# A hybrid SSD and Conformer layer on one core: the issue order of all queues, up to the up projection, from a table in the source

## The chip, the cores and the metric

The kernel runs on one core of a Trainium2 chip. The metric is the device time of one execution in microseconds (us), lower being better. The core has a matrix engine (TensorE, PE in the profile), a vector engine (VectorE, DVE), an activation engine (ScalarE, ACT), a general engine (GpSimd, POOL) and a queue that issues the DMA transfers (SyncE, SP). Each of them works through its own list of instructions in order, and an instruction that needs the result of another engine waits for that engine's semaphore at the head of its list, with everything queued behind it.

## The reference

One inference step of a trunk layer over 128 context tokens and 512 latent tokens, width 1024, in float32:

```python
mod = jax.nn.silu(cond) @ prm["w_ada"] + prm["b_ada"]
sh1, sc1, g1, sh2, sc2, g2 = [m[:, None, :] for m in jnp.split(mod, 6, axis=-1)]
h = rms_norm(x, prm["norm_mix_pre"]) * (1 + sc1) + sh1
proj = h @ prm["w_in"]
z, xbc, dt_raw, cf_in = jnp.split(proj, [...], axis=-1)
xbc = jax.nn.silu(dwconv1d(xbc, prm["w_ssd_conv"], prm["b_ssd_conv"]))
...
y_f, s_f = ssd_chunked(xs, dt_f, a_f, b_mat, c_mat, init_f)
y_b, s_b = ssd_chunked(jnp.flip(xs, 1), jnp.flip(dt_b, 1), a_b, ...)
y = y_f + jnp.flip(y_b, 1) + xs * prm["d_skip"][:, None]
y_ssd = rms_norm(y * jax.nn.silu(z), prm["ssd_norm"])
cf_a, cf_g = jnp.split(cf_in, 2, axis=-1)
u = cf_a * jax.nn.sigmoid(cf_g)
u = dwconv1d(u, prm["w_cf_conv"], prm["b_cf_conv"])              # 31 taps
u = jax.nn.silu(layer_norm(u, prm["cf_ln_g"], prm["cf_ln_b"]))
mix = jnp.concatenate([y_ssd, u], axis=-1) @ prm["w_out"]
x = x + g1 * rms_norm(mix, prm["norm_mix_post"])
h = rms_norm(x, prm["norm_ffn_pre"]) * (1 + sc2) + sh2
up = h @ prm["w_ffn_up"]                                          # 1024 -> 5632
up = dwconv1d(...) if rows is None else dwconv2d(...)             # 3x3 on latent tokens
f_gate, f_val = jnp.split(up, 2, axis=-1)
f = (jax.nn.silu(f_gate) * f_val) @ prm["w_ffn_down"]             # 2816 -> 1024
x = x + g2 * rms_norm(f, prm["norm_ffn_post"])
```

The SSD scan (`ssd_chunked`) works in chunks of 128 tokens: one for the context, four for the latent tokens, in both directions, for 16 heads. The outputs are the context and latent tokens and the final SSD states of the context.

## The kernel before

Features lie on the 128 partitions and the 640 tokens (128 context, 512 latent) on the free axis. A matrix product in float32 precision is made of three matmuls in the faster `fp32r` type: weights and inputs are each split into a high part (a copy rounded by ScalarE, L165 for weights) and a low part (the difference, L167, mostly on GpSimd), and `mm3` (L261 to 268) issues high x high, high x low and low x high, each for two column halves of 384 and 256 tokens.

The stages follow one another, and each overlaps with its neighbours:

1. The adaLN product for the first half of the modulation (L276 to L297), the first products of the input projection and of dt (L268, L360, L399).
2. The B and C columns, their three-tap conv (`conv3_silu`, L421 to L430), the preparation of dt (`dtprep`, L452 to L517) and the masked products of C and B (`cb_masks`, L528, L532).
3. Eight steps p = 0 to 7, one for each pair of heads, `ssd(p)`: tokens and states (`ssd_tokens`, `ssd_states`, L563 to L592), the broadcast of the decays by TensorE into two PSUM banks in turn (L635), from which ScalarE reads them with a bias (L641; L638 on VectorE in the last step), exponentials (L649), products with the mask (L652), the y_off product (L659, L661), the chunk product (L670, L675) and the tail `ssd_tail` (L686 to L696). Beside a step run the input projection for the next z, gate and value columns (L268), the gate (L704), the gated value (L709) and the 31-tap conv of one channel block, `conv31(p)`: most taps on VectorE as one pass each over 655 columns in PSUM (L725).
4. The layer norm of the conv's result (L764, L326 to L341, L834), its SiLU (L839), the group norm of y, and the splits of the results for the output projection (L840, L852, L862).
5. The output projection, partly run ahead in the last steps, and its sums of squares; the class `Mid` (L989 on) turns its result into x2 and the input of the second sub-layer, by column half: `msum` and `rsqrt` (L326, L341), `spread` (L334), `x2` (L1012 to L1015), `xsum`, `all_h2` (L1032, L1034, L1039).
6. The up projection (L1116 for the first products, then L268) with the 3x3 conv on ScalarE, VectorE and GpSimd (L1084, L1094), the gate, and the down projection.

What sets the order: the program is written as a list of instructions in emission order, and the Tile framework's scheduler turns it into one list for each engine. It goes by priorities, dependencies and a timeline of its own, and hints in the source change what it picks. There are three kinds: `tc.issue_after(ins)` puts an instruction behind another, `tc.high_priority()` prefers a group, and `tc.high_priority(offset=-3000)` around `conv31` makes its taps fill in where nothing else is ready. The hints stand at the first products (L399), `conv31` (L712), the layer norm (L833: passes 4 to 7 behind the low parts of earlier ones; L836: the SiLUs behind the last step's exponentials), the group norm (L879), `rsqrt` (L995), `all_h2` (L1050), and from L1170 on in the up and down projections.

Of the kernel before, what the change touches and what calls it, by code (L numbers as in the profile page):

```python
# [1 line left out]

# [7 lines left out]
AF = mybir.ActivationFunctionType  # L10
# [7 lines left out]
T = L + C  # L18
# [19 lines left out]
for _name, _w in (("b_ada", 48), ("g_mix_pre", 8), ("g_mix_post", 8), ("g_ffn_pre", 8),  # L38
# [3 lines left out]
    _COLS[_name] = (_n, _n + _w)  # L42
    _n += _w
NPRM = _n


@with_exitstack
def hybrid_layer_kernel(ctx: ExitStack, tc: tile.TileContext, xT, ct, prm, cst, wrest, wdt, idhl_d, wada1, wada2, win,
# [212 lines left out]
    def mm3(pt, hi, lo, j, xh, xl, first, last, halves=(0, 1), places=None):  # L261
        w1 = hi[:, j * P:(j + 1) * P]
        w2 = lo[:, j * P:(j + 1) * P]
        for i, (w, x) in enumerate(((w1, xh), (w1, xl), (w2, xh))):
            for h in halves:
                o, c0, c1 = HALF[h]
                out = places[h] if places else pt[:, o:o + c1 - c0]
                last_mm[0] = te.matmul(out, w, x[:, c0:c1], start=first and i == 0, stop=last and i == 2)  # L268
# [40 lines left out]
    def ada_half(i, ws, now=True):  # L309
        pt = psq(i % 2)  # L310
        for kc, w in enumerate(ws):
            for j in range(4):
                te.matmul(pt[32 * j:32 * j + 32, 0:P], cts[:, kc, :], w[:, j * P:(j + 1) * P],  # L313
                          start=kc == 0, stop=kc == KD - 1, tile_position=(0, 32 * j))
        r = sm.tile([P, P], F32, tag="adar", name=nm("adar"), bufs=1)
        ac.activation(r, pt[:, 0:P], AF.Copy)
        b = 8 * ADA_REST[i // 2] + 4 * (i % 2)
        to_modv = ada_out(r, pt, P, (b, b + 1, b + 2, b + 3))
        if now:
            to_modv()  # L320
        return to_modv
# [16 lines left out]
    def rsqrt_mean(pt, o, seg):  # L338
        r = sm.tile([P, 160], F32, tag="rsm", name=nm("rsm"), bufs=1)
        ac.activation(r[:, 0:seg], pt[:, o:o + seg], AF.Sqrt, bias=epsc, scale=1.0 / D)  # L340
        ve.reciprocal(r[:, 0:seg], r[:, 0:seg])  # L341
        return r
# [487 lines left out]
    def layer_norm(pr):  # L830
        los = []
        for p in range(NPAIR):
            with tc.issue_after(los[(p - 4) // 2].ins) if p > 3 else nullcontext():  # L833
                ve.tensor_tensor(uc[p], uc[p], pr[:, 192:192 + T], MUL)  # L834
            hi, lo = slot(USLOT[2 * p], F32R), slot(USLOT[2 * p + 1], F32R)
            with tc.issue_after(ssd_exp[0].ins):  # L836

                for o in (hi, uc[p]):
                    ac.activation(o, uc[p], AF.Silu, scale=prm_col("ln_g", p), bias=prm_col("ln_b", p))  # L839
            r = (ve if p % 2 else gp).tensor_tensor(lo, uc[p], hi.bitcast(F32), SUB)  # L840
            if p % 2:
                los.append(r)
            mix[8 + p] = hi, lo
# [32 lines left out]
    prior = None  # L876
    for p in range(NA, NPAIR):
        for h in range(2):
            with tc.issue_after(prior.ins) if prior else nullcontext():  # L879
                prior = ve.scalar_tensor_tensor(tp[p][:, h * HT:(h + 1) * HT], tp[p][:, h * HT:(h + 1) * HT],  # L880
                                                prm_col("ssd_g", p), pry[h][:, 0:HT], MUL, MUL)
# [106 lines left out]
    class Mid:  # L988
# [178 lines left out]

    def up_conv_of(i, v, out):
        conved[i] = out
        with tc.issue_after(prior[0].ins) if prior[0] else nullcontext():  # L1170
            prior[0] = up_conv(v, ups[i][1] * NF + ups[i][0], out)
# [28 lines left out]
    for i in range(HEAD, 2 * NF):  # L1200
        q, half = ups[i]
        w = get_unit(unit_of["up", i])
        pt = next_ps()
        for k in range(KD):
            mm3(pt, *w, k, *h2[k], k == 0, k == KD - 1)
        if i == 2 * NF - 1:
            break
        if i == 2 * NF - 2:
            held = pt
            continue  # L1210
        up_conv_of(i, view(pt), acc_slot(q, half))
# [26 lines left out]
    with tc.issue_after(prior[0].ins):
        for q in range(NDIR, 8):
            split_f(q)  # L1240
    with tc.issue_after(split_ins[0].ins):
        up_conv_of(2 * NF - 2, view(held), acc_slot(NF - 1, 0))
    for q in range(8, 12):
        split_f(q, gp)
    with tc.issue_after(prior[0].ins):
        for q in range(12, EARLY):
            split_f(q)
    with tc.issue_after(split_ins[0].ins):
        up_conv_of(2 * NF - 1, view(pt), acc_slot(NF - 1, 1))
# [87 lines left out]
    with tc.issue_after(last_mm[0].ins):
        r = out_sums(0)
    with tc.issue_after(r.ins):
        down_mm(m, 1, pt, range(k1, k2))  # L1340
    with tc.issue_after(last_mm[0].ins):
        r = out_spread(0)
    with tc.issue_after(r.ins):
        down_mm(m, 1, pt, range(k2, NF))
# [121 lines left out]
```

## Time and profile before

| | before |
|---|---|
| median of 3 runs | 1014.41 us (1012.62 to 1015.32) |
| the profiled execution | 1013.18 us |
| its span, first to last instruction | 1011.4 us |
| TensorE busy | 970.7 us (96%) |
| VectorE busy | 736.7 us (73%) |
| GpSimd busy | 589.1 us (58%) |
| ScalarE busy | 457.5 us (45%) |
| mean granted TensorE clock | 0.990 |

Reading the profile: a line of the timeline begins with the start and the duration in us, then engine, line of the source, operation, the output and the inputs by the program's names, their shapes, and the number of instructions that the line stands for. In square brackets stands the idle time of the engine just before it and what released it. `ps` and `pq` are PSUM tiles, `wh` and `wl` the split weights, `H`, `S` and `T` slots in SBUF. In a table of windows, the numbers in parentheses are instructions, and `PEclk` is the granted TensorE clock as a share of full speed.

### The profile page before, as it was taken

The numbers are of one execution on the slowest core, as the hardware profiler recorded it, in microseconds if no ns is written. First come the engines' busy times: TensorE is split into PE (matmuls) and PEld (weight loads), VectorE is DVE, ScalarE is ACT, GpSimd is POOL, SyncE is SP. The second block draws the span as 40 slices with busy tenths as digits, with TensorE's granted clock in tenths as the row PEclk, the third lists the DMA queues.
The fourth block names the chain that finished last, engine by engine and source line by source line (L and its number), as shares of the span: only waits on it lengthen the run. The fifth ranks groups of instructions, "written<-read, shape, count | busy, mean of one in ns | idle before, by whom it ended". The sixth has DMA issues, their size and how long they took to land.

```text
span 1011.4 us, 18834 instructions
## 1 busy us (share of the span) xinstructions
PE 970.7 (96%) x7655; PEld 936.7 (93%) x7655; DVE 736.7 (73%) x1093; ACT 457.5 (45%) x766; POOL 589.1 (58%) x426
## 2 busy tenths in 40 slices
PE   5999999999999989999989999999999999999995
PEld 2799999999999978899979999999999999999995
DVE  3789999989999988672286798899888888500004
ACT  6344556564563857842354753332332336321221
POOL 3333978888787786443473696544444546444444
PEclk9999999999999999999999999999999999999998
DMA  9622121121212111559463422122222221322212
GB/s 344 239 70 84 55 88 63 54 81 57 74 43 65 41 49 41 168 160 391 158 201 109 147 66 81 63 84 83 64 85 84 64 84 58 91 82 74 78 38 104
DMA packets 42934, 102.76 MB, mean 102 GB/s; under 512 B 4832, under 2 KB 12768, under 8 KB 42848
## 3 DMA queue, kind: packets, MB, share of 16 engines
q1 hardware_dynamic: 42848, 101.56, 30.3%
q8 instruction: 60, 0.98, 0.4%
q14 instruction: 26, 0.21, 0.1%
HBM read 97.87 MB, written 3.67 MB: 100 GB/s over the span
## 4 chain that ended last, share of the span: by engine, by line
PE 84%; DVE 7%; ACT 3%; POOL 2%; issue 2%; DMA 2%; SPq 0%; POOLq 0%; ACTq 0%; DVEq 0%
PE ps L268 69%; PE ps L1116 3%; PE pq L268 2%; PE pq L670 2%; PE pq L313 2%; DVE T L764 1%; PE pq L659 1%; DVE ps L725 1%; POOL wl L167 1%; PE pq L577 1%; DMA prms<-in_prm 1%; PE pq L294 1%; PE pq L635 1%; DMA T<-in_wada 1%; DVE M L1014 1%
## 5 line engine op out<-in xcount | busy, mean ns | idle before, releaser
L167 POOL TENSOR_TENSOR wl<-wr,wh 128x1024 fp32r<-128x1024 f32 (+3 forms) x127 | 291.9, 2299 | 293.7 <-ACT wh L165 286.9
L268 PE MATMUL ps<-H,wh 128*128 128x384 f32 (+1 forms) x1636 | 322.7, 311 | 5.2 <-DVE M L425 2.2
L165 ACT ACTIVATE wh<-wr 128x1024 fp32r<-128x1024 f32 (+3 forms) x131 | 131.7, 1006 | 346.7 <-PE ps L268 210.0
L268 PE MATMUL ps<-T,wh 128*128 128x384 f32 (+1 forms) x1472 | 273.3, 306 | 1.8 <-ACT S L1084 1.8
L268 PEld LDWEIGHTS ps<-H,wh 128*128 128x128 f32 x1636 | 250.0, 189 | 9.6 <-issue 4.5
L1094 DVE SCALAR_TENSOR_TENSOR S<-ps,prms,S 128x441 f32<-128x441 f32 (+2 forms) x336 | 233.5, 695 | 31.7 <-ACT S L1084 21.2
L268 PEld LDWEIGHTS ps<-T,wh 128*128 128x128 f32 x1472 | 219.4, 188 | 2.1 <-ACT S L1084 2.1
L725 DVE SCALAR_TENSOR_TENSOR ps<-u,prms,ps 128x655 f32<-128x655 f32 x223 | 200.8, 900 | 9.9 <-ACT ps L722 5.4
L268 PE MATMUL ps<-H,wl 128*128 128x384 f32 (+1 forms) x818 | 194.7, 310 | 0.0
L268 PE MATMUL ps<-T,wl 128*128 128x384 f32 (+1 forms) x736 | 166.9, 306 | 0.0
L268 PEld LDWEIGHTS ps<-H,wl 128*128 128x128 f32 x818 | 129.0, 188 | 1.6 <-issue 1.2
L268 PEld LDWEIGHTS ps<-T,wl 128*128 128x128 f32 x736 | 113.1, 188 | 0.0
L341 DVE RECIPROCAL rsm<-rsm 128x160 f32<-128x160 f32 (+2 forms) x9 | 7.3, 815 | 138.2 <-ACT rsm L340 138.2
L268 PE MATMUL ps<-S,wh 128*128 128x384 f32 (+1 forms) x420 | 87.1, 311 | 1.9 <-DVE M L927 1.4
L268 PEld LDWEIGHTS ps<-S,wh 128*128 128x128 f32 x420 | 65.7, 188 | 4.4 <-issue 2.7
L268 PE MATMUL ps<-S,wl 128*128 128x384 f32 (+1 forms) x210 | 54.2, 308 | 0.3 <-POOL wl L167 0.3
L641 ACT ACTIVATE S<-pq,ACM 128x128 f32<-128x128 f32 x140 | 41.1, 374 | 18.9 <-PE pq L635 18.7
L1084 ACT ACTIVATE S<-ps,prms 128x640 f32<-128x640 f32 x42 | 36.5, 869 | 0.0
L268 PEld LDWEIGHTS ps<-S,wl 128*128 128x128 f32 x210 | 34.9, 188 | 0.5 <-POOL wl L167 0.5
L592 POOL TENSOR_TENSOR S<-S,stmp 128x128 f32<-128x128 f32 x36 | 18.6, 516 | 15.2 <-ACT S L581 11.3
L1197 POOL TENSOR_TENSOR H<-S,S 128x640 f32<-128x640 f32 x16 | 25.3, 1582 | 0.0
L652 POOL TENSOR_TENSOR S<-S,M 128x640 f32<-128x640 f32 x14 | 22.1, 1576 | 4.4 <-ACT S L649 4.4
(353 smaller groups left out, 1279.6 us busy)
## 6 DMA issues: line engine op xcount, KB each, us to landing
wr<-in_wup SPq DMA_DIRECT2D x44, 512.0 KB, 3.4
wr<-in_win SPq DMA_DIRECT2D x36, 512.0 KB, 3.4
T<-in_wada SPq DMA_DIRECT2D x49, 256.0 KB, 5.4
wr<-in_wdown SPq DMA_DIRECT2D x16, 512.0 KB, 3.4
wr<-in_wout SPq DMA_DIRECT2D x13, 512.0 KB, 3.4
H<-in_wada SPq DMA_DIRECT2D x23, 256.0 KB, 5.4
S<-in_wada SPq DMA_DIRECT2D x16, 256.0 KB, 5.4
wr<-in_wdown SPq DMA_DIRECT2D x8, 384.0 KB, 3.1
```

Source lines behind the costliest of these rows:

```text
L165: ac.activation(hi[:, :n], raw[:, :n], AF.Copy)
L167: lo_eng.tensor_tensor(lo[:, :n], raw[:, :n], hi[:, :n].bitcast(F32), SUB)
L268: last_mm[0] = te.matmul(out, w, x[:, c0:c1], start=first and i == 0, stop=last and i == 2)
L313: te.matmul(pt[32 * j:32 * j + 32, 0:P], cts[:, kc, :], w[:, j * P:(j + 1) * P], start=kc == 0, stop=kc == KD - 1, tile_position=(0, 32 * j))
L641: ac.activation(r[:, c * P:(c + 1) * P], pb[:, (c - c0) * P:(c - c0 + 1) * P], AF.Relu, scale=-1.0, bias=ACM[:, c, row:row + 1])
L652: (ve if i % 2 or last else gp).tensor_tensor(r, r, cbm[g][d], MUL)
L670: te.matmul(py[64 * h:64 * h + 64, i * P:(i + 1) * P], xd[d][:, c * P + 64 * h:c * P + 64 * h + 64], rs[h, d][:, c * P:(c + 1) * P], start ...
L725: ve.scalar_tensor_tensor(acc, u[:, j:j + UO], w(j), acc, MUL, ADD)
L1084: ac.activation(out, v, AF.Identity, bias=prm_col("ffn_b", i), scale=w(1, 1))
L1094: ve.scalar_tensor_tensor(ob, vl[:, r0 + a - 1:r1 + a - 1, q0 + b - 1:q1 + b - 1], w(a, b), ob, MUL, ADD)
L1116: te.matmul(pt[:, o:o + c1 - c0], w[k] if i in (1, 2) else w[:, k * P:(k + 1) * P], x[:, c0:c1], start=k == 0 and j == 0, stop=k == KD - 1 ...
L1197: gp.tensor_tensor(f_raw[q], a, b, MUL)
```

## The change

All hints listed above are taken out, and so are those of the up and down projections. In their place a dictionary `ORDER` holds, for each of the five queues, the order of all its instructions, each named by its place in the emission order of that queue: 6733 for PE, 1093 for VectorE, 748 for ScalarE, 422 for GpSimd, 294 for SP. At the end of the kernel's source a new function chains them:

```python
def issue_in_order(tc):
    given = {e: [] for e in ORDER}
    for i in tc.nc.cur_bb.bb.instructions:
        if i.opcode != "TilePoolBoundary":
            given[str(i.engine).split(".")[-1]].append(i)
    behind = mybir.DependencyInfo(mybir.DependencyClass.NoSync, mybir.DependencyReason.DATA)
    for e, text in ORDER.items():
        order = []
        for word in text.split():
            a, _, b = word.partition("-")
            order += range(int(a), int(b or a) + 1)
        assert sorted(order) == list(range(len(given[e]))), e
        for a, b in zip(order, order[1:]):
            tc.add_manual_dep(given[e][b], given[e][a].name, behind, reason="order")
```

A dependency of the kind `NoSync` orders two instructions of one queue for the scheduler and puts no semaphore into the program. The beginning of the table, and the diff where hints go:

```diff
+ORDER = {
+    "PE": """
+0-31 36-47 32-35 48-68 102 69-72 103 73-76 104-105 116-117 77-100 118 101 119 106-110 120-132 161 175
+111-115 162 133-159 176 163 177 164 160 178-179 165 180 187-199 181-183 166-168 200-218 169-171 184-186
...
             for k in (k0, k0 + 1):
-                with tc.issue_after(turned[0].ins) if s == 2 else nullcontext():
-                    mm3(pt, whi, wlo, k, h_hi[k], h_lo[k], k == 0, k == KD - 1)
+                mm3(pt, whi, wlo, k, h_hi[k], h_lo[k], k == 0, k == KD - 1)
...
     def conv31(p):
-        with tc.high_priority(offset=-3000):
-            conv31_sum(p)
+        conv31_sum(p)
...
-            with tc.issue_after(los[(p - 4) // 2].ins) if p > 3 else nullcontext():
-                ve.tensor_tensor(uc[p], uc[p], pr[:, 192:192 + T], MUL)
+            ve.tensor_tensor(uc[p], uc[p], pr[:, 192:192 + T], MUL)
...
-            with tc.issue_after(ssd_exp[0].ins):
-
-                for o in (hi, uc[p]):
-                    ac.activation(o, uc[p], AF.Silu, scale=prm_col("ln_g", p), bias=prm_col("ln_b", p))
+            for o in (hi, uc[p]):
+                ac.activation(o, uc[p], AF.Silu, scale=prm_col("ln_g", p), bias=prm_col("ln_b", p))
...
         def rsqrt(self):
-            with tc.high_priority():
-                self.r = rsqrt_mean(self.pt, 0, self.n // 4)
+            self.r = rsqrt_mean(self.pt, 0, self.n // 4)
...
             if k < KD:
-                with tc.issue_after(done[-1].ins) if done else nullcontext():
-                    mid[h].h2_raw(k)
+                mid[h].h2_raw(k)
...
+    issue_in_order(tc)
```

The same kind of edit is made at L879, L1170, L1223, L1226, L1238 to L1251, L1311 and L1337 to L1343. The statements that compute, their operands and their tiles are the same in both kernels.

More of the change, by code (lines that the diff above doesn't have):

```diff
@@ L1 @@
-from contextlib import ExitStack, nullcontext
+from contextlib import ExitStack
 import concourse.bass as bass
@@ new lines @@
+1538 1205 1539-1540 1531-1532 1541 1533 1542-1543 1534 1201-1202 1535-1537 1203-1204 1544-1547 1206-1208
+1548 1209-1212 1549-1550 1213-1216 1551-1562 1217-1221 1563-1566 1222 1233-1236 1223-1232 1586-1596
+1429-1432 1597 1567 1598-1599 1568-1573 1434 1574-1580 1600-1602 1581-1585 1436 1603-1632 1634-1641 1633
+1438 1642-1647 1433 1648-1651 1440 1435 1652-1662 1437 1663-1678 1439 1679-1681 1733-1738 1441 1739-1750
+1442-1445 1751 1446 1752-1761 1448 1762-1780 1447 1449-1456 1829 1457 1830-1852 1458 1461-1464 1459
@@ new lines @@
+1853-1855 1460 1856-1863 1465-1467 1481-1482 1468-1475 1483-1484 1476-1480 1864-1873 1485-1486 1489
+1487-1488 1874 1781-1800 1875 1801-1812 1876 1813-1815 1682 1816-1823 1684 1824-1828 1683 1686 1877-1882
+1688 1883-1903 1685 1904-1910 1687 1911-1918 1689 1919-1924 1976-2024 1690-1693 2025-2026 1694 2027-2031
+1695 2032-2040 1696 2041-2052 1697-1699 2053-2058 1701-1704 2059-2065 1709-1711 1700 2066-2071 1712
+2072-2078 1705 2079 1729-1732 2080 1706 2081-2082 1707-1708 2083-2093 1713-1728 2094-2102 1925 2103-2107
@@ new lines @@
+2120-2125 2108-2109 1926 2126-2132 1928 2133-2134 2110-2119 1927 2135-2150 1929 2151-2159 2219 2160
+2220-2225 2161-2162 2226-2228 1930 2163-2164 2229-2230 2165-2166 2231 1931 2232-2233 2167 2234 1932
+2235-2266 1937 1933-1936 2267-2311 2365 2312-2314 1938-1941 1944-1946 1942 2366 1947 1943 2369 1952-1955
+1948-1951 2370 2413-2441 1956-1971 2442 1972-1975 2443 2168 2444 2169 2445-2451 2170 2452-2464 2172
+2465-2466 2171 2467-2472 2174 2173 2473-2482 2175 2483-2499 2176 2500-2502 2180 2177-2179 2315-2318
@@ new lines @@
+2788-2799 2815-2823 2800-2810 2824-2839 2811-2812 2866-2884 2848 2885-2896 2849 2897 2850 2840-2844
+2851-2859 2899 2845 2860 2900-2901 2861-2865 2846 2813-2814 2902-2907 2847 2908-2912 2898 2913-2915 2950
+2916-2940 2951 2941-2944 2952 2945-2948 2953-2982 3016-3020 2983-2988 3021-3022 2989-3010 3023-3024
+3011-3014 3148-3149 3025-3033 3150-3155 3034 3082 3156 3083-3089 3035-3043 2949 3044 3090 3049-3075 3045
+3076-3080 3046 3091 3015 3092 3047-3048 3081 3093 3115-3126 3094 3127-3130 3095-3096 3131-3134 3097-3099
@@ new lines @@
+3725-3730 3566-3567 3731-3732 3568-3570 3700 3733 3701-3704 3734-3736 3705-3712 3628 3713-3715 3629-3630
+3676-3681 3631-3650 3652-3654 3737-3738 3651 3655-3675 3682-3699 3716-3723 3739-4115 4117-4137 4116
+4138-5604 5653-5671 5605-5652 5672-5714 5749-5751 5715-5720 5752-5772 5721-5748 5773-6655 6721-6724
+6656-6720 6725-6732""",
+    "DVE": """
+0 3-6 47 154 1-2 9-12 14 13 15 7-8 19-20 24 16 21 25 22-23 26 17-18 29-30 34-35 31-32 36 33 27-28 37-38
+42-43 39-41 44-46 71-78 101-102 79 103 80 104 48 81 49 82 62 83 50 84 51 85 105-107 86 108 52-55 87 113-114
@@ new lines @@
+626-627 632-633 630-631 634-766 1070 767-1063 1066-1068 1064-1065 1069 1071-1080 1082 1081 1083-1092""",
+    "Activation": """
+1 0 2-10 16 33 15 11-12 18 17 19 21-22 20 24 23 25 13 26-27 14 28-29 46 43 30-31 47 49 32 50 54 44 57 55 51
+45 56 48 58-59 35-36 60 37-38 34 39 41 40 66 61 42 67 64 52 103 65 68 53 62-63 107 104 69-71 108-109 72-77
+97 78-82 110 83-87 99 88-90 114 98 93 91 115 92 95 94 111 96 102 116 148 101 147 151 100 152-154 117-121
+112-113 141 160 122-125 158 105 127-128 126 129-131 143 132-134 163 161 155 142 162 164 159 137 166 135 106
@@ new lines @@
+593 591-592 598 594 604 599-600 609 605 616 610-611 618 617 621 619-620 623 622 626 624-625 628 627 631
+629-630 633 632 636 634 638 635 637 641 639 643 640 642 646 644 648 645 647 651 649 653 650 652 656 654 658
+655 657 661 659 663 660 662 666 664 690 668 665 667 671 669 672 670 677 673-676 678 682 679 688-689 680 683
+694 681 686 684-685 695 687 691-692 696-697 693 698 704 699-703 708 705-707 709-710 714 711-713 715-716 720
+717-719 721-722 726 723-725 727-728 732 729-731 733-734 738 735-737 739-747""",
+    "Pool": """
@@ new lines @@
+336 328 342-343 337 345-346 344 348-349 347 351-352 350 354-355 353 357-358 356 360-361 359 363-364 362
+366-367 365 369-370 368 372-373 371 375-376 374 377-379 382 380 383-384 381 385-387 389 388 390-391 393 392
+394-395 397 396 398-399 401 400 402-403 405 404 406-407 409 408 410-421""",
+    "SP": """
+0-22 25-49 56 23-24 50-55 62-64 57-58 65 69-71 60-61 72 59 73-74 78-79 67-68 66 80-81 85-87 76-77 75 88
+92-95 83-84 82 99-102 90-91 105 89 106-108 97-98 109 96 110-113 103-104 114 118 115 121 126-129 116 130 195
@@ L878, in hybrid_layer_kernel @@
         for h in range(2):
-            with tc.issue_after(prior.ins) if prior else nullcontext():
-                prior = ve.scalar_tensor_tensor(tp[p][:, h * HT:(h + 1) * HT], tp[p][:, h * HT:(h + 1) * HT],
-                                                prm_col("ssd_g", p), pry[h][:, 0:HT], MUL, MUL)
+            prior = ve.scalar_tensor_tensor(tp[p][:, h * HT:(h + 1) * HT], tp[p][:, h * HT:(h + 1) * HT],
+                                            prm_col("ssd_g", p), pry[h][:, 0:HT], MUL, MUL)
         mix[p] = split_act(("S14", "S2", "S3")[p - 5], ("S1", "S4", "S5")[p - 5], tp[p], ve if p % 2 else gp)
@@ L1169, in up_conv_of @@
         conved[i] = out
-        with tc.issue_after(prior[0].ins) if prior[0] else nullcontext():
-            prior[0] = up_conv(v, ups[i][1] * NF + ups[i][0], out)
+        prior[0] = up_conv(v, ups[i][1] * NF + ups[i][0], out)
     acc_slot = lambda q, half: slot({(1, 0): "S16", (2, 1): "S17"}.get((q, half), f"S{10 + 2 * half + q % 2}"))
@@ L1222, in hybrid_layer_kernel @@
         if i == 11:
-            with tc.issue_after(last_mm[0].ins):
-                g2_rest = ada_half(7, ada_w2, now=False)
+            g2_rest = ada_half(7, ada_w2, now=False)
         if i == 14:
-            with tc.issue_after(prior[0].ins):
-                g2_rest()
+            g2_rest()
         if i == 5:
@@ L1235, in split_f @@
         f_hl[q] = split_act(*ht[q - NDIR], f_raw[q], lo_eng)
[L1238 to L1242, printed above, removed]
+    for q in range(NDIR, 8):
+        split_f(q)
+    up_conv_of(2 * NF - 2, view(held), acc_slot(NF - 1, 0))
     for q in range(8, 12):
         split_f(q, gp)
[L1245 to L1249, printed above, removed]
+    for q in range(12, EARLY):
+        split_f(q)
+    up_conv_of(2 * NF - 1, view(pt), acc_slot(NF - 1, 1))
     finish(NF - 1)
-    with tc.issue_after(prior[0].ins):
-        for q in range(EARLY, NF):
-            split_f(q)
+    for q in range(EARLY, NF):
+        split_f(q)
     gg2 = small("asc", "gg2", 64)
@@ L1310, in out_apply @@
             rs = out_rs[half][:, c0:c1] if e is gp else out_pr[half][:, 128:128 + c1 - c0]
-            with tc.issue_after(prior[e].ins) if e in prior else nullcontext():
-                e.tensor_tensor(mg[i][:, c0:c1], mg[i][:, c0:c1], rs, MUL)
+            e.tensor_tensor(mg[i][:, c0:c1], mg[i][:, c0:c1], rs, MUL)
             prior[e] = e.tensor_tensor(mg[i][:, c0:c1], mg[i][:, c0:c1], x2[i][:, c0:c1], ADD)
@@ L1336, in hybrid_layer_kernel @@
     down_mm(m, 1, pt, range(k1))
[L1337 to L1344, printed above, removed]
+    r = out_sums(0)
+    down_mm(m, 1, pt, range(k1, k2))
+    r = out_spread(0)
+    down_mm(m, 1, pt, range(k2, NF))
     out_apply(0)
```

82 lines of the change are left out of this document (added).

## The prediction

> **What bounds the kernel now.** I read the first and fourth parts of the page, then busy time by window, then the waits of TensorE (PE), then the places of the largest waits in time.
>
> ```profile
> span 1011.4 us, 18834 instructions
> PE 970.7 (96%) x7655; PEld 936.7 (93%) x7655; DVE 736.7 (73%) x1093; ACT 457.5 (45%) x766; POOL 589.1 (58%) x426
> PE 84%; DVE 7%; ACT 3%; POOL 2%; issue 2%; DMA 2%; SPq 0%; POOLq 0%; ACTq 0%; DVEq 0%
> ```
>
> PE is busy for 970.7 of 1011.4 us, so an order that only moves work can win from 40.7 us of idle PE and from stretches at a low clock. The windows (columns: length, then busy time of PE, of its weight loads, VectorE (DVE), ScalarE (ACT), GpSimd (POOL), then the granted clock) say how much of that lies where the table differs:
>
> ```profile
> 28.79:575.00 546.21, 528.29 (x4468) 503.38 (x4468) 444.04 (x632) 295.37 (x551) 349.44 (x278) 0.99 0.32 108
> 50.00:350.00 300.00, 294.67 (x2183) 290.53 (x2180) 280.66 (x371) 166.84 (x327) 219.29 (x182) 1.00 0.20 66
> 384.00:434.00 50.00, 48.93 (x431) 43.95 (x430) 38.46 (x45) 38.74 (x51) 29.36 (x24) 1.00 0.34 109
> 650.00:700.00 50.00, 50.00 (x351) 50.00 (x350) 46.04 (x76) 15.48 (x18) 23.13 (x12) 1.00 0.24 78
> 69.75:73.16 3.41, 1.64 (x11) 1.67 (x12) 3.41 (x8) 1.70 (x2) 0.00 (x0) 1.00 0.00 0
> 356.47:359.88 3.41, 1.36 (x25) 1.36 (x26) 3.41 (x6) 1.07 (x3) 2.62 (x5) 1.00 0.46 135
> 359.88:363.29 3.41, 3.41 (x21) 3.08 (x18) 3.41 (x4) 0.00 (x0) 3.08 (x4) 0.50 0.00 0
> 527.13:530.55 3.42, 1.61 (x14) 0.93 (x13) 3.42 (x4) 2.44 (x5) 2.35 (x1) 1.00 0.98 338
> 530.55:533.96 3.41, 3.05 (x10) 3.05 (x11) 3.41 (x8) 2.11 (x3) 0.00 (x0) 0.50 0.98 381
> ```
>
> Set beside the emission order, the table gives PE the order it already has up to the instruction that starts at 29.5 us and from about 565 us on; VectorE, ScalarE and GpSimd part and meet again inside the same stretch, and SP's list of DMA issues is the same throughout. The up projection (row 650 to 700: PE busy for all of it, 351 matmuls, 0.1425 us each) and the down projection therefore stay as they are. In 28.79 to 575, PE is idle for 546.21 - 528.29 = 17.9 us, and two windows of 3.41 us run at clock 0.50, losing about 1.7 us each: 17.9 + 3.4 = 21.3 us is all that can be won. The waits of PE there name most of it (total, times, longest):
>
> ```profile
> PE pq L670 <- DVE S L661: 2.4, 1, 2.4
> PE ps L268 <- DVE M L425: 2.2, 1, 2.2
> PE ps L1116 <- DVE T L1039: 2.0, 2, 1.7
> PE pq L577 <- ACT S L620: 1.8, 2, 1.6
> PE ps L268 <- ACT u L704: 1.5, 1, 1.5
> PE ps L268 <- ACT T L862: 1.5, 2, 0.9
> PE ps L268 <- DVE M L927: 1.4, 1, 1.4
> PE ps L268 <- ACT wh L165: 0.5, 1, 0.5
> PE pq L326 <- ACT S L689: 0.4, 1, 0.4
> ```
>
> **The change, part by part.** No instruction, transfer or semaphore is added or removed; the hints that go were orders between instructions of one queue, and the table replaces them. What it moves: some 987 PE, 198 VectorE, 200 ScalarE and 101 GpSimd instructions, by 133 places at most. PE changes between kinds of matmul as often as before, so I cost the moves themselves at nothing. Each wait is then judged by what the new list puts in front of the waiting instruction and of its producer.
>
> *The y_off product of head pair 6 (L670).*
>
> ```profile
> 355.78 0.36 PE L635 MATMUL ps<-HL,idr 128*128 128x256 f32 x1
> 358.52 2.42 PE L670 MATMUL pq<-S,S 128*64 128x128 f32 x32 [2.38 <-DVE S L661]
> 357.79 0.67 DVE L661 TENSOR_TENSOR S<-S,pq 128x512 f32<-128x512 f32 x1
> 359.20 0.67 DVE L661 TENSOR_TENSOR S<-S,pq 128x512 f32<-128x512 f32 x1
> 364.59 7.49 DVE L725 SCALAR_TENSOR_TENSOR ps<-u,prms,ps 128x655 f32<-128x655 f32 x8
> ```
>
> PE has nothing else queued and waits 2.38 us for a VectorE product. The table puts 28 matmuls of the output projection (L268, weights split ahead, inputs done before the wait begins) in front: 28 x 0.1425 = 4.0 us of work, which covers 2.38. The idle is what the half clock follows: all windows here lie on one grid of 3.41 us, and 1.36 us busy of 3.41 precedes the one at 359.88. Without the gap PE is busy for the whole of it, so 2.4 + 1.7 = 4.1 us go. Bounds: 0 (the L670s merely wait later, on VectorE, which runs conv taps back to back, 0.94 us each in the last row) and 4.1. I take 4.1. Late next: the layer norm chain on VectorE and ScalarE in 384 to 434. It is fed by those taps, not by PE, so I give 2 us back there (bounds 0 to 5). The cover for that is thin: PE is 48.93 of 50 us busy in that window.
>
> *The gate's evacuation (L704), 1.5 us.*
>
> ```profile
> 283.50 2.40 POOL L167 TENSOR_TENSOR wl<-wr,wh 128x1024 fp32r<-128x1024 f32 x1
> 285.86 2.15 POOL L687 TENSOR_TENSOR T<-T,T 128x640 f32<-128x640 f32 x1
> 288.05 0.74 ACT L689 ACTIVATE S<-T 128x640 f32<-128x640 f32 x1 [0.24 <-POOL T L687]
> 289.56 1.04 ACT L165 ACTIVATE wh<-wr 128x1024 fp32r<-128x1024 f32 x1
> 290.50 0.74 ACT L704 ACTIVATE u<-ps 128x512 f32<-128x512 f32 x2
> ```
>
> L704 stands behind L689, which waits for GpSimd's L687, itself behind a weight split of 2.40 us, and behind a weight split of its own (1.04). The table puts L686 and L687 ahead of the split on GpSimd and L704 ahead of L165: 2.40 + 1.04 exceeds 1.53, so 1.5 goes. The splits it passes feed matmuls several microseconds on.
>
> *The conv3 taps of B (L425), 2.2 us; the mid chain (L927, L1039), 1.4 + 2.0 us and the second half clock.*
>
> ```profile
> 64.19 2.31 DVE L475 TENSOR_TENSOR T<-T 128x160 f32<-128x160 f32 x1
> 520.30 0.75 DVE L341 RECIPROCAL rsm<-rsm 128x96 f32<-128x96 f32 x1 [1.74 <-ACT rsm L340]
> 522.28 0.61 DVE L1032 SCALAR_TENSOR_TENSOR HL<-M,gs,pq 128x384 f32<-128x384 f32 x1 [0.95 <-PE pq L334]
> 528.15 2.70 DVE L1039 SCALAR_TENSOR_TENSOR T<-U,modv,T 128x384 fp32r<-128x384 f32 x1
> 528.09 2.35 POOL L167 TENSOR_TENSOR wl<-wr,wh 128x1024 fp32r<-128x1024 f32 x1 [2.23 <-ACT wh L165]
> ```
>
> For L425 about ten small passes of the dt preparation, the 2.31 us one among them, go behind; against it PE reaches the waiting matmul 12 places (1.7 us) sooner. Bounds 0.4 to 1.5; I take 1. In the mid stage the sums and the spread that start the x2 chain (L326, L334) go 28 PE places forward, 28 x 0.1425 = 4.0 us, and the third L1039, which costs 2.70 us where its neighbours take 0.6, goes four VectorE places forward (4 x 0.6 = 2.4). That covers the 1.4 and the 2.0. The half clock at 530.55 follows a window with 1.61 us of busy PE; one with 1.64 (69.75 to 73.16) was not followed by any. So a little less idle suffices, and 1.7 goes too: 5.1 in all, of which I take 4.5 (bounds 0 to 5.1).
>
> The Trainium skill, "TensorE: Matmul & The Clock Gate" (section "HAM oscillation — how this bites in real kernels"), asks that PE never idle for more than some 3.4 us; by that rule gaps of 2.38 us would cost no clock, and the sum below would be 3.4 us smaller. The rows above disagree: less than half busy in one 3.41 us window was enough.
>
> *Smaller ones.* L862's 1.5: three ScalarE passes leave the queue ahead of it, 1. L620's 1.6: a weight split of 1.04 us leaves the queue ahead of it, but the L616 that feeds it is pushed up to its reader, 0.5. L689 and L165 (0.4 + 0.5): fifty L268 go ahead, 0.9. The first products, 29 to 55 us: several adaLN transposes and passes move both ways while weights still land, 0 (bounds -2 to 1).
>
> *What it brings in.* The rows of the decay broadcast:
>
> ```profile
> 157.26 0.34 PE L635 MATMUL pq<-HL,idr 128*128 128x384 f32 x1
> 158.42 0.28 PE L635 MATMUL pq<-HL,idr 128*128 128x256 f32 x1
> 286.92 0.89 ACT L641 ACTIVATE S<-pq,ACM 128x128 f32<-128x128 f32 x3 [4.17 <-PE pq L635]
> ```
>
> Two banks take turns, and each must be read by two or three L641 (0.89 for three) before its next L635. In the order of before, most L635s of one bank stand 26 to 28 PE places apart and four stand 12 or less; in the table sixteen stand 7 to 12 apart, which is 1.0 to 1.7 us, against 0.3 + 0.9 and whatever ScalarE has in front. If a turn waits, the L635 stops PE's queue with the ready L268s behind it. The waits of PE on L641 before come to one:
>
> ```profile
> PE ps L635 <- ACT H L641: 0.7, 1, 0.7
> ```
>
> So I let a tight turn cost between 0 and 0.7; at 0.25 for the twelve new ones I take 3 us (bounds 0 to 8.4).
>
> *Sum.* 4.1 + 1.5 + 1 + 4.5 + 1 + 0.5 + 0.9 = 13.5; less 3 and 2 leaves 8.5 us. The profiled execution took 1013.18 us (span 1011.4); 1013.2 - 8.5 = 1004.7. It is 1.2 under the median of 1014.41, so against the runs the sum says 1005.9: 1006.
>
> **Rivals.**
> 1. *No net change.* VectorE is 280.66 of 300 us busy from 50 to 350 us and has the conv taps of every pair to run; if it and not PE sets the pace between the stages, PE only waits elsewhere. Then just the mid stage (4.5) and L704 (1.5) pay, less 3 for the new waits: 1011.4; with 3 more lost on the layer norm chain 1014.4. For: the row 50 to 350. Against: PE is idle there for only 5.3 us, so there is slack on VectorE at most of the places.
> 2. *The gate stays.* One mechanism: scattered gaps still add up to over 1.8 us in one grid window at both places. Each costs 1.7: 1005.9 + 3.4 = 1009.3. For: 1.61 against 1.64 shows how near the edge is, and where the grid lies differs from run to run for all the trace says. Against: at L670 the gap is covered outright. The skill's page named above gives the same 1009.3, for another reason.
> 3. *Slower: the bank turns.* With six turns moved together in each of seven head pairs, 42 turns at c us cost 42c. The gains less the give-back are 11.5, so over 0.3% slower begins at (11.5 + 3.0) / 42 = 0.35 us a turn; at 0.5 the time is 1014.4 - 11.5 + 21 = 1023.9. For: a weight split (1.04) just ahead of the L641s would make such a wait at once. Against: ScalarE is 166.84 of 300 us busy there, and the page shows it waiting for L635, not the reverse.
>
> Speaking for rival 1 in the mid stage is a rule too: the Trainium skill, "Advanced Engine Details and Errata" (section "VectorE Performance Modes"), says that GpSimd and VectorE passes that use the second port block each other. The trace agrees, as 2.70 us beside a GpSimd pass of 2.35 shows; a fixed order does not fix when two engines meet.
>
> **How the numbers follow.** My forecast (998 to 1008.5) gets 0.51, rival 2 0.16, rival 1 0.23 (two thirds of it within 0.3%), rival 3 0.10. 0.3% is 3.0 us, about what a measurement of this kernel can tell from no change: 1011.4 to 1017.4 is the same. Faster: 0.51 + 0.16 + 0.08 = 0.75; the same 0.15; slower 0.10. The range goes from 13.5 and two microseconds of unlisted idle won with nothing lost, 1014.4 - 15.5 = 999, to rival 1's upper end, 1014.4.
>
> **What would show it.** In the profile after: no L670 wait near 356 us and clock 1.00 in the windows after it; L704's row before L165 and no 1.5 us wait of L268 on it; L1116 waits on L1039 under 0.5 us. New waits of PE in "L635 <- ACT L641" would be the cost I put at 3; over 12 there is rival 3. If PE's idle time between 29 and 565 us falls but the span does not, the sum was wrong in kind: the work would have been slowed, not the waits moved. PE's stretch from there to the end should take what it took before.

## The result, and the profile after

The changed kernel takes 1021.59 us (median of 6 runs, 1019.46 to 1023.99), the kernel before 1012.84 (6 runs, 1009.18 to 1015.32): 8.75 us more, a ratio of 1.0089 with a 95% interval of 1.0063 to 1.0114. The profiled execution took 1019.46 us, its span 1017.7. The prediction said 1006, and 999 to 1014.4: wrong in sign.

From the page of the changed kernel:

```profile
span 1017.7 us, 18770 instructions
PE 979.4 (96%) x7655; PEld 931.9 (92%) x7655; DVE 705.8 (69%) x1093; ACT 452.0 (44%) x764; POOL 588.1 (58%) x426
```

TensorE is idle for 1017.7 - 979.4 = 38.3 us, against 40.7 before: less waiting, as forecast. But the same 7655 matmuls keep it busy for 8.7 us longer. (`x` counts records; a float32 matmul leaves two of them here, so the 32 instructions of one adaLN product are 64 records.) So the waits alone do not tell what was lost; what counts is how long PE takes from one fixed instruction to another. At many places of PE's queue both orders have issued the same set of instructions and stand at the same one. The next two tables of windows (length, then busy time of PE, its weight loads, VectorE, ScalarE, GpSimd, clock) go from such an instruction to the next, first in the kernel before, then in the changed one:

```profile
48.41:128.71 80.30, 78.05 (x550) 76.50 (x550) 73.39 (x110) 39.30 (x74) 41.24 (x32) 1.00 0.22 75
128.71:259.88 131.17, 131.17 (x997) 129.76 (x997) 123.50 (x156) 79.89 (x156) 109.92 (x92) 1.00 0.21 67
259.88:302.19 42.31, 39.23 (x296) 37.67 (x295) 39.65 (x52) 21.06 (x43) 32.40 (x29) 1.00 0.18 57
346.88:369.03 22.15, 18.03 (x134) 16.13 (x132) 21.87 (x25) 10.56 (x26) 19.57 (x19) 0.92 0.10 30
369.03:441.01 71.98, 70.31 (x581) 63.60 (x579) 54.49 (x69) 55.90 (x90) 44.57 (x35) 1.00 0.31 100
441.01:492.28 51.27, 51.27 (x620) 47.98 (x620) 21.85 (x34) 13.70 (x23) 19.39 (x12) 1.00 0.84 293
492.28:516.92 24.64, 23.27 (x193) 22.26 (x192) 13.36 (x18) 11.43 (x18) 17.00 (x11) 1.00 0.39 125
516.92:575.25 58.33, 53.73 (x518) 49.87 (x515) 40.43 (x94) 33.59 (x68) 27.20 (x19) 0.97 0.46 155
575.25:1000.26 425.01, 424.54 (x3014) 423.64 (x3013) 274.11 (x432) 144.12 (x191) 220.17 (x117) 1.00 0.24 74
```

```profile
48.91:128.75 79.84, 78.45 (x552) 75.61 (x550) 66.31 (x107) 36.23 (x68) 32.57 (x24) 1.00 0.21 68
128.75:262.87 134.12, 133.33 (x998) 130.19 (x996) 118.51 (x158) 81.64 (x163) 112.86 (x97) 1.00 0.21 69
262.87:303.48 40.61, 39.52 (x296) 37.81 (x295) 35.97 (x50) 21.93 (x46) 34.81 (x31) 1.00 0.18 60
348.57:367.65 19.08, 16.27 (x133) 14.56 (x132) 17.33 (x22) 11.04 (x24) 17.12 (x20) 1.00 0.16 49
367.65:440.62 72.97, 71.28 (x580) 63.45 (x579) 53.54 (x77) 54.90 (x90) 46.93 (x36) 1.00 0.27 90
440.62:499.83 59.21, 57.86 (x621) 48.07 (x620) 13.39 (x29) 12.04 (x21) 18.63 (x12) 1.00 0.74 259
499.83:525.63 25.80, 23.88 (x193) 22.35 (x193) 15.88 (x22) 11.94 (x21) 17.12 (x13) 1.00 0.41 134
525.63:581.58 55.95, 52.93 (x517) 48.44 (x516) 37.41 (x90) 31.01 (x64) 26.76 (x19) 1.00 0.48 158
581.58:1006.54 424.96, 424.49 (x3014) 423.39 (x3013) 274.65 (x433) 144.94 (x192) 220.64 (x117) 1.00 0.23 75
```

Three stretches where waits were to go did gain: 42.31 to 40.61, 22.15 to 19.08, 58.33 to 55.95. The up and down projections did not move. Most of the loss is in one row: the first part of the output projection goes from 51.27 to 59.21 us for the same 620 records, +7.94. A part of the SSD steps (131.17 to 134.12) adds 2.95, and the stretch behind the large loss (24.64 to 25.80) another 1.16.

What is different inside that row shows in PE's timeline. Before (L313 is the adaLN product, 128*32 tiles in float32; L268 the output projection, 128*128 in fp32r):

```profile
467.44 0.51 PE L268 MATMUL ps<-H,wh 128*128 128x384 f32 x2
467.78 0.34 PE L268 MATMUL ps<-H,wl 128*128 128x384 f32 x1
468.05 1.30 PE L313 MATMUL pq<-H,cts 128*32 128x128 f32 x40
469.17 0.84 PE L313 MATMUL pq<-T,cts 128*32 128x128 f32 x24
469.94 0.62 PE L268 MATMUL ps<-S,wh 128*128 128x384 f32 x2
470.39 0.34 PE L268 MATMUL ps<-S,wl 128*128 128x384 f32 x1
```

After (L465 and L420 are the same two lines):

```profile
463.57 0.45 PE L420 MATMUL ps<-S,wh 128*128 128x384 f32 x1
463.94 0.43 PE L465 MATMUL pq<-T,cts 128*32 128x128 f32 x8
464.30 0.44 PE L420 MATMUL ps<-S,wl 128*128 128x384 f32 x1
464.67 0.43 PE L465 MATMUL pq<-T,cts 128*32 128x128 f32 x8
465.03 0.62 PE L420 MATMUL ps<-S,wh 128*128 128x384 f32 x2
486.59 0.86 PE L465 MATMUL pq<-H,cts 128*32 128x128 f32 x24 [0.36 <-issue]
495.85 0.45 PE L420 MATMUL ps<-S,wl 128*128 128x384 f32 x1 [0.90 <-POOL wl L319]
```

Read the starts. Before, all 64 records of one adaLN product run together, 468.05 to 469.94, 0.03 us each. The way in costs 0.27 from the last L268, where a matmul of 384 columns alone takes 0.175, and the first two matmuls behind it take 0.45 instead of 0.35. After, one matmul and eight records take 464.30 - 463.57 = 0.73 us, where 0.175 + 8 x 0.03 = 0.41 would be their own time: 0.32 for going there and back. No row shows it as idle time, since the duration of each row (0.43 to 0.45) reaches past the start of the next. The last two rows are the two largest waits of PE in this stretch. In this stretch the table cuts six adaLN products into 22 blocks; before they were 8.

### The profile page after: what moved, and what is told of

Its sections match the earlier page's. It is cut to its first block, busy times and chain, and to the rows that moved or that the text cites. A ratio compares the mean times of both kernels' runs of the same rounds, so it can differ in the third digit from the quotient of the medians.

```text
span 1017.7 us, 18770 instructions
## 1 busy us (share of the span) xinstructions
PE 979.4 (96%) x7655; PEld 931.9 (92%) x7655; DVE 705.8 (69%) x1093; ACT 452.0 (44%) x764; POOL 588.1 (58%) x426
## 4 chain that ended last, share of the span: by engine, by line
PE 53%; ACT 3%; DVE 2%; issue 2%; DMA 2%; POOL 1%; POOLq 0%; ACTq 0%; SPq 0%
PE ps L420 45%; PE ps L1261 2%; PE pq L420 2%; PE pq L465 1%; DMA wr<-in_wout 1%; ACT T L987 1%; DMA H<-in_wada 1%; DVE S L1239 1%; ACT wh L317 1%; DVE T L1185 0%; PE pq L478 0%; PE pq L486 0%; DMA wr<-in_wrest 0%; PE ps L478 0%; POOL wl L319 0%
## 5 line engine op out<-in xcount | busy, mean ns | idle before, releaser
L420 PE MATMUL ps<-H,wh 128*128 128x384 f32 (+1 forms) x1636 | 333.0, 313 | 3.4 <-ACT H L405 1.4
L420 PE MATMUL ps<-T,wh 128*128 128x384 f32 (+1 forms) x1472 | 273.1, 306 | 1.2 <-DVE S L1242 1.2
L420 PEld LDWEIGHTS ps<-H,wh 128*128 128x128 f32 x1636 | 253.3, 188 | 13.0 <-issue 5.0
L420 PEld LDWEIGHTS ps<-T,wh 128*128 128x128 f32 x1472 | 219.3, 188 | 1.8 <-ACT H L1264 1.4
L420 PE MATMUL ps<-H,wl 128*128 128x384 f32 (+1 forms) x818 | 198.7, 311 | 0.0
L420 PE MATMUL ps<-T,wl 128*128 128x384 f32 (+1 forms) x736 | 166.9, 306 | 0.0
L420 PEld LDWEIGHTS ps<-H,wl 128*128 128x128 f32 x818 | 131.1, 188 | 1.9 <-issue 1.7
L420 PEld LDWEIGHTS ps<-T,wl 128*128 128x128 f32 x736 | 113.0, 188 | 0.0
L420 PE MATMUL ps<-S,wh 128*128 128x384 f32 (+1 forms) x420 | 90.5, 314 | 0.6 <-ACT wh L317 0.2
L420 PEld LDWEIGHTS ps<-S,wh 128*128 128x128 f32 x420 | 66.5, 188 | 5.5 <-issue 3.0
L420 PE MATMUL ps<-S,wl 128*128 128x384 f32 (+1 forms) x210 | 55.5, 312 | 0.9 <-POOL wl L319 0.9
L420 PEld LDWEIGHTS ps<-S,wl 128*128 128x128 f32 x210 | 35.2, 188 | 2.2 <-POOL wl L319 1.2
L743 POOL TENSOR_TENSOR S<-S,stmp 128x128 f32<-128x128 f32 x36 | 21.4, 596 | 14.4 <-issue 7.0
```

The lines of the kernel that those rows point to most:

```text
L743: gp.tensor_tensor(now, now, tmp, ADD)
```

## The experiments

All tables below are made of the two orders; `before` and `table` in the sketches are the two kernels' lists of a queue, and PE places are counted from the start of its list. Ratios are against the kernel before, timed on the same chip.

**The order of before, given by the table.** (Sketch against the changed kernel.)

```diff
-ORDER = {"PE": """0-31 36-47 32-35 48-68 102 69-72 103 73-76 104-105 116-117 77-100 118 101 ...
+ORDER = {"PE": """0-31 36-47 32-35 48-68 102 69-72 103 73-76 104-105 116-117 77-80 106-107 118-119 ...
```

> The kernel before's own order, written into the table (all hints out, all five queues chained). Every theory that lays the loss on the order itself expects no change against before: 0 within 3 us. If giving the order by a table costs something by itself (other semaphores, other tile slots), it shows here as +6 to +9 us.

Measured 1012.14 us, ratio 0.9992 (0.9979 to 1.0006). Giving the order by a table costs nothing that these runs can tell; what the changed kernel lost, it lost by the order. Its trace has a second use: the same order, another execution. From 48 us on it repeats the trace of before within 0.5 us, stretch by stretch, except in the one around L670 and the one behind:

```profile
345.63:366.12 20.49, 16.36 (x133) 14.62 (x132) 20.38 (x24) 10.56 (x26) 18.86 (x19) 1.00 0.10 33
366.12:438.72 72.60, 70.30 (x580) 63.60 (x579) 55.86 (x70) 55.89 (x90) 45.18 (x35) 1.00 0.32 99
357.26 1.97 PE L788 MATMUL pq<-S,S 128*64 128x128 f32 x32 [2.38 <-DVE S L779]
```

PE waits the same 2.38 us (L788 is L670), but the clock stays at 1.00 and the stretch takes 20.49 instead of 22.15. Four more traces below have this order at that place (the two with the adaLN and the square products cut up, the output projection only, the mid stage alone): each waits 2.37 or 2.38 us, keeps the clock at 1.00 and takes 20.5. So the half clock of before's profile there came in one execution of six. The profiled spans differ by only 6.3 us, where the medians differ by 8.75, mostly because the profiled execution of the changed kernel was its fastest of six, 1019.46 against a median of 1021.59.

**The table up to the output projection only.**

```diff
-PE = table
+PE = table[:2757] + before[2757:]        # the other queues likewise, at their places of that time
```

> The table's order on all engines up to the output projection (PE place 2757, 441 us in the trace of before), the order of before from there on. In the two traces the same instruction at that place starts 0.4 us earlier in the changed kernel. Theory A (the loss is made in the output projection, by cutting the adaLN products into small blocks between the fp32r matmuls): -0.4 us against before, within 3 us. Rival B (the loss comes from the bank turns of the decay broadcast in the SSD steps, rival 3 of the prediction): slower than before by 5 to 9 us.

1014.04 us, 1.0018 (1.0003 to 1.0033): 1.5 us slower than before where -0.4 was expected, probably because the expectation took before's half clock for granted: against the second trace of before's order the changed kernel reaches that place later, at 440.62 instead of 438.72. The bank turns (rival 3) would have made 5 to 9. So gains and losses ahead of 441 us nearly cancel, and the 7 to 8 us are made behind it.

**The adaLN products in one block each.**

```diff
-  ... 2815-2823 (9 of a product) ... 2824-2839 ... 2840-2844 ... 2845 ... 2846 ...
+  ... 2815-2846 (all 32, at the place of the last) ...
```

> The table, but on PE the six adaLN products of the output projection (32 instructions each) stand in one block each, at the place of their last instruction; 32 changes between these products and other matmuls fewer. Theory A: the trace has 0.27 us from a 384-column matmul into a 128*32 product where a matmul alone takes 0.175, and 0.21 from the product back where products follow each other at 0.04: 0.26 a round trip, 16 round trips, -4.2 us against the changed kernel, and up to 1 more for a wait on weights: 1016.5 to 1017.5. Rival C (the loss there is waits for the split weights, 0.5 and 1.1 us, and the blocks are innocent): within 1 us of the changed kernel, 1021, or slower, since the products now all run late.

1017.60 us, 1.0053 (1.0036 to 1.0071): 4.0 us less than the changed kernel, just above what theory A said, and partly by luck: theory A's 0.26 a round trip was too small (next run). Rival C is out. The stretch takes 56.38 us, 2.8 less, where 16 round trips at 0.34 would give 5.4. One of the blocks now waits for its weights eight records at a time, five times for 1.4 us in sum, behind these waits comes a window of 3.4 us at half clock (1.7 us lost), and the late split stays:

```profile
442.00:498.38 56.38, 54.00 (x621) 48.90 (x620) 13.48 (x29) 12.11 (x21) 18.72 (x12) 0.97 0.78 271
464.55 0.43 PE L460 MATMUL pq<-T,cts 128*32 128x128 f32 x8 [0.36 <-DMA T<-in_wada]
465.39 0.59 PE L460 MATMUL pq<-T,cts 128*32 128x128 f32 x8 [0.41 <-DMA T<-in_wada]
494.41 0.45 PE L415 MATMUL ps<-S,wl 128*128 128x384 f32 x1 [0.92 <-POOL wl L314]
```

**The order of before, with these products cut up.**

```diff
-  ... 2815-2846 2848-2867 2847 ...
+  ... 2815-2818 2848-2849 2819-2822 2850-2851 2823-2826 2852-2853 2827-2830 2854-2855 ...
```

> The order of before on all engines, but on PE each of the six adaLN products of the output projection is cut into eight blocks of four with two matmuls between: 80 changes of kind more than before (40 round trips), nothing else moved. Theory A: 40 x 0.26 = +10.4 us against before, 1023. Rival C: no wait is added, so within 3 us of before.

1025.79 us, 1.0132 (1.0108 to 1.0155), 13.7 above the run of before's own order. The stretch is busy from end to end:

```profile
438.84:503.85 65.01, 65.01 (x620) 44.25 (x620) 21.31 (x33) 13.44 (x23) 19.71 (x12) 1.00 0.71 225
```

65.01 - 51.27 = 13.7 us for 40 round trips: 0.34 each, and not one wait. The price is shown; the expectation's 0.26 left out the second matmul behind a block. What the price is made of inside the engine, no row shows.

**The same cutting with square tiles.**

```diff
-  ... 627-634 959-981 ...
+  ... 627-631 959 632 960 633 961 634 962-981 ...        # L659, 128*128, float32
```

> The order of before, but on PE seven of the sixteen y_off products (L659 in before; 128*128 tiles, float32, four instructions each) have three fp32r matmuls put between their four instructions: 40 changes of type more (184 to 224), no change of tile shape more. If what costs is the change of tile shape (128*32 against 128*128): no change, within 3 us of before. If it is the change of type (float32 against fp32r) at the price seen for the adaLN products (0.26 to 0.34 a round trip, 20 of them): +5 to +7 us.

1012.90 us, 1.0002 (0.9987 to 1.0017). From 129 to 347 us, which holds 34 of the 40 changes, first before and then with the cuts:

```profile
128.71:346.88 218.17, 215.09 (x1630) 211.64 (x1630) 205.59 (x263) 126.47 (x251) 175.54 (x149) 1.00 0.20 63
128.78:346.76 217.98, 214.91 (x1631) 211.53 (x1630) 204.89 (x263) 126.34 (x251) 175.15 (x149) 1.00 0.20 63
```

So the change of type costs nothing here. Nor is it the shortness of a piece that costs: two pieces of a square product, 0.22 us each, with one matmul of 384 columns between them (L779 is L659):

```profile
147.64 0.38 PE L779 MATMUL pq<-M,AT 128*128 128x128 f32 x2
148.04 0.38 PE L779 MATMUL pq<-M,AT 128*128 128x128 f32 x2
```

From start to start 0.40 us, where the piece alone takes 0.22 (three in a row take 0.67, from 146.63 to 147.30) and the matmul 0.175: nothing is left over. What costs is going between 128*128 and 128*32 tiles.

**The table in the output projection only.**

```diff
-PE = before
+PE = before[:2757] + table[2757:3183] + before[3183:]        # the other queues likewise
```

> The order of before, with the table's order on all engines from 441 to 492 us alone, the first part of the output projection with its adaLN products. Theory A (the loss is made there): 7.7 to 8 us slower than before, which is the stretch's loss in the trace of the changed kernel: 1020. If that loss came from what the earlier stages hand over: under +3 us.

1021.58 us, 1.0099 (1.0072 to 1.0126): this stretch alone costs as much as the whole table, whose other gains and losses come out nearly even. It takes 59.22 us, as in the changed kernel (59.21). Part of the cost falls behind it: the next stretch, in before's order again, takes 26.23 us instead of 24.64 and 24.27 in the two traces of that order.

**The table, with before's PE order in the output projection.**

```diff
-PE = table
+PE = table[:2757] + before[2757:3183] + table[3183:]         # the other queues keep the table
```

> The table on all engines, but PE has the order of before in its places 2757 to 3183 (441 to 492 us in the trace of before): the adaLN products stand in 8 blocks there instead of 22. ScalarE, VectorE, GpSimd and the DMA queue keep the table. If PE's order makes the loss of that stretch: the stretch gets back 7.8 us, 1014 against 1021.6 of the changed kernel; 1.1 us less (1015) if the late weight split at 496 us (PE waits for GpSimd) belongs to the other queues. If the other queues' order makes half of it or more: 1017.5 or above.

1015.65 us, 1.0024 (1.0008 to 1.0040): 5.9 us less than the changed kernel, nearest to the 1015 that was expected if PE's order makes the loss and the late split belongs to the other queues.

```profile
441.69:495.84 54.15, 51.73 (x621) 48.06 (x620) 12.68 (x30) 12.60 (x21) 19.28 (x12) 1.00 0.81 284
456.12 0.33 PE L419 MATMUL pq<-csts,adar 128*128 128x128 f32 x1 [0.72 <-ACT adar L459]
491.40 0.45 PE L411 MATMUL ps<-S,wl 128*128 128x384 f32 x1 [1.70 <-POOL wl L310]
```

Of the 7.94 us, 59.21 - 54.15 = 5.1 go back with PE's order. The other 2.9 stay with the table's order on the other queues: 0.72 + 1.70 of them stand there as waits for ScalarE and GpSimd.

**Three stretches that gained, transplanted.**

```diff
-PE = before
+PE = before[:1652] + table[1652:1903] + before[1903:2207] + table[2207:2303] + before[2303:3360] + table[3360:]
 # the other queues likewise
```

> The order of before, with the table's order on all engines in three stretches alone (places of before's trace): 260 to 302 us, 347 to 369 us, and from 517 us on. By the stage times of the traces so far these win 1.4 to 1.7 us, 2.9 us (1.3 where the half clock at 360 us does not come anyway), and 2.4 us. If the stages' times add up: -5 to -6.5 us against before, 1006 to 1008. If stages borrow from one another (a gain in one is given back in the next): within 3 us of before.

1021.72 us, 1.0094 (1.0070 to 1.0117): a miss by 14 us. The stretch that was to gain 1.5 lost 4.3, and PE waits 3.63 us for the decay banks:

```profile
260.61:307.20 46.59, 41.86 (x297) 40.08 (x296) 36.64 (x50) 22.30 (x46) 31.81 (x29) 0.93 0.17 52
292.23 0.69 PE L756 MATMUL pq<-HL,idr 128*128 128x384 f32 x1 [3.63 <-ACT S L762]
```

Pair 6 and the stretch behind it, 23.24 and 77.52 us, lost as well. The account that fits is that the queues stand at other distances from each other in the two orders, so that a stretch of one need not fit between two of the other; no run separates it from others. Only the last stretch, from 517 us on, behaved as it did in the table.

**Head pair 6 alone, on all queues, and on PE alone.**

```diff
 # all queues, 347 to 369 us
-PE = before
+PE = before[:2207] + table[2207:2303] + before[2303:]
 # PE alone: the 28 matmuls ahead of L670
-  ... 1956-1971 2413-2422 1972-1975 2423-2442 ...
+  ... 2413-2440 1956-1975 2441-2442 ...
```

> The order of before, with the table's order on all engines from 347 to 369 us alone (head pair 6, 28 matmuls ahead of the y_off product L670). By the prediction's step (2.4 us of idle and 1.7 of half clock): -2.9 in the trace's stage, -4.1 at most against before; -1.3 to -2.4 if the half clock does not come in most runs of before. If the gain is given back on the layer norm chain up to 434 us: 0.

> The order of before on all engines, but on PE 28 matmuls of the output projection (L268) go ahead of the y_off product L670 of head pair 6, where PE waited 2.4 us; nothing else moves. The prediction's step by itself: -2.4 us (-4.1 with the half clock). If the L670s are then late for VectorE and the decay broadcast of pair 7, the wait comes back at the next L635 and behind: between -1 and +2 us.

1016.22 us, 1.0038 (1.0024 to 1.0053), and 1012.92 us, 1.0016 (1.0000 to 1.0033). Neither gains. With the PE move alone, in a profiled execution 2.5 us above the median of that kernel (L753 is L635 of before):

```profile
346.52:365.12 18.60, 16.40 (x133) 14.65 (x132) 18.23 (x21) 10.96 (x27) 16.82 (x16) 1.00 0.12 37
365.12:443.01 77.89, 73.32 (x580) 66.55 (x579) 58.33 (x74) 55.60 (x89) 47.27 (x38) 0.96 0.29 94
372.41 0.44 PE L753 MATMUL pq<-HL,idr 128*128 128x384 f32 x1 [2.79 <-ACT S L759]
```

The stretch gains 20.49 - 18.60 = 1.9 us and the next one loses 77.89 - 72.60 = 5.3: the wait moves from L670 to the next decay broadcast, 2.79 us, and 6.8 us at half clock follow it here, 3.4 of the 5.3. Without them the gain and the loss would be equal.

**The mid stage alone, and a version of three edits.**

```diff
 # mid stage, all queues
+PE = before[:3360] + table[3360:]
 # and in the version of three edits also
+16 matmuls ahead of L670 of pair 6; the two adaLN products of 2 + 30 in one block each
```

> The order of before, with the table's order on all engines from 517 us on alone (the mid stage: sums, spread, x2 and the first products of the up projection). The prediction gave this stage 4.5 us, half clock included; the traces of two other orders with this part give 2.4 to 2.8 by stage. If it holds alone: -2.4 to -2.8 us against before, 1010. If it depends on what the stages ahead hand over: within 1 us of before.

> The order of before with three edits: the table's mid stage from 517 us on (as in the run for the mid stage), 16 of the matmuls ahead of L670 of pair 6 instead of 28, and the two adaLN products that before cuts into 2 and 30 instructions in one block each (4 changes of tile shape fewer). If all three hold: -2.6 for the mid stage, -2.3 for 16 x 0.1425 us of cover at L670, -0.6 for the blocks: -5.5 us, 1007. If the wait at L670 moves on: -3 us, 1010.

1010.52 us, 0.9992 (0.9974 to 1.0009), not to be told from before; and 1010.09 us, 0.9981 (0.9968 to 0.9995), about 2 us under before: the only one of the twelve whose interval stays below 1, and only just, which one of twelve may do by chance. The mid stage of the first, and the mid stage and the output projection of the second:

```profile
514.96:571.03 56.07, 52.88 (x519) 48.65 (x516) 39.10 (x94) 32.32 (x67) 27.61 (x21) 1.00 0.48 164
518.47:573.95 55.48, 52.93 (x519) 48.65 (x515) 38.48 (x94) 32.42 (x67) 26.74 (x19) 1.00 0.48 161
443.32:494.06 50.74, 50.74 (x621) 48.12 (x620) 21.20 (x33) 13.55 (x23) 19.75 (x12) 1.00 0.82 287
```

58.33 to 56.07 and 55.48 for the mid stage, and 51.27 to 50.74 for four changes of shape fewer. Four of the eight traces with before's order of the mid stage have a half clock near its L1039, and none of the six with the table's. The step at pair 6 gave nothing here either: its stretch gains 20.49 - 18.69 = 1.8, the next one takes 77.26.

## Why the prediction was wrong

**The step that failed** is the first sentence on the cost of the moves: "PE changes between kinds of matmul as often as before, so I cost the moves themselves at nothing." It does not. Over PE's whole list the changes of tile shape go from 98 to 138, and those around the adaLN products of L313 from 22 to 50; all 28 more are in the output projection, 14 round trips. At 0.34 (from cutting up before) that is 4.8 us, and the two waits of the stretch (0.36 and 0.90) bring it to 6.0 of the 7.94; exchanging PE's order gave 5.1 back. The 2 us left are spread and stay unassigned. The Trainium skill, "TensorEngine Tiling (Array Packing)", section "Tiling Modes", says in its key properties that changing the tiling mode drains the engine. The trace agrees that the change costs time, 0.34 us a round trip. It is the rule that spoke against the change, and the prediction weighed others.

The prediction also looked for losses in the wrong column. It asked what PE's idle time could lose; the loss came as busy time, in a stretch (441 to 492 us) where before PE is never idle and which it therefore did not look at. "What would show it" named the case, that idle time falls and the span does not, but the prediction gave it no chance.

Point by point:
- **L670 of pair 6** (4.1 forecast): 22.15 to 19.08 in the two profiles, but 1.7 of it is the half clock that the same order need not have. Against the second trace of before's order the gain is 1.4, with 0.4 given back behind (72.60 to 72.97). And the 28 matmuls ahead are not what earns it: by themselves they gain 1.9 and lose at least as much behind. That a half clock follows this wait held in one execution of six. What the table does with the other queues there belongs to it; which of their moves matter was not taken apart.
- **L704 and L620** (1.5 + 0.5): 42.31 to 40.61, 1.7. Right; the two waits there went from 1.53 to 0.22 and from 1.55 to 0.78.
- **B's conv3 taps** (1): no gain that shows. The wait of 2.25 us went, a new one of 1.39 for ScalarE stands at 50.58, and the stretch takes 79.84, where the second trace of before's order has 79.86.
- **L862, L689, L165 and the give-back** (1.9 less 2): 71.98 to 72.97, a loss of 1.0 instead of 0.1 in the two profiles; but the same order took 72.60 in its second trace, so the loss is not clear of that spread.
- **The mid chain** (4.5 with L927 and half clock): 24.64 + 58.33 to 25.80 + 55.95, 1.2. The longer first stretch comes with the order of the output projection (26.23 with the table there only). The half clock went, and L1116 waits 0.7 us for L1039 instead of 2.0 (under 0.5 was forecast). The wait for L927 went too, and another in the same stretch took its place:

```profile
520.13 0.37 PE L478 MATMUL pq<-T,ones 128*32 128x96 f32 x8 [1.66 <-DVE M L1158]
```

  (L1158 is L1012 of before, the first pass of x2, and L478 is L326.) With before's order ahead of it, the stage from 517 us on gained 2.3 (mid stage alone) and 2.9 (three edits) against 58.33, the half clock included.
- **The new waits in the SSD steps** (3): 131.17 to 134.12 is 2.95, the right size by luck, for the wrong reason. It repeats: the second trace of before's order has 131.16, the table up to the output projection 134.45. The waits of PE from 100 to 350 us in the changed kernel are:

```profile
PE pq L728 <- ACT S L771: 0.8, 1, 0.8
PE pq L599 <- ACT S L792: 0.7, 1, 0.7
PE ps L420 <- ACT u L855: 0.2, 1, 0.2
```

  One wait on the decay banks, 0.7, and none in L786 itself (L635 of before): rival 3, which has the sign of the result, did not happen. Four more changes of shape there, to 128*64 tiles (0.7 us if a round trip costs 0.34 there too, which no run measured), and one wait are half of the 2.95; what the other half is stays open.
- **Rival 2** (the gate stays): in the changed kernel's profile the clock is 1.00 in every stretch shown, so it did not in that execution.

## What to carry to other kernels

Count the changes of tile shape on TensorE before and after any reordering, and keep small column-tiled products in few blocks, where their weights are there in time: here a round trip cost 0.34 us, as much as two matmuls of 384 columns, and no row shows it as a wait. Compare two orders by the time between instructions at which both have issued the same set, not by idle time. Do not count on a stretch of one schedule behind another predecessor: moved between others, a gain of 1.5 us became a loss of 4.3, while the mid stage kept its gain.

## What the runs showed of the hardware

- TensorE's change from 128*128 to 128*32 tiles and back costs 0.34 us (13.7 us for 40), shared by the way in (0.27 where 0.175 is the matmul's own), the way back and the second matmul behind it; the change between float32 and fp32r in square tiles costs nothing that shows (217.98 against 218.17 us with 34 changes of type more).
- The same wait of 2.4 us was followed by 3.41 us at half clock in one execution and by none in five others with the same order at that place, a difference of 1.7 us in that stretch (22.15 against 20.49). One profile cannot tell which is usual.
